# Gate and up strips of a SwiGLU block in pairs: seven block products in place of eight, in a float32 decoder kernel

## The chip, the cores and the metric

The kernel runs on one core of a Trainium2 chip. The core has a matrix engine (TensorE, PE in the profile; its loading of the stationary operand is shown apart as PEld), a vector engine (VectorE, DVE), an activation engine (ScalarE, ACT), GpSimd (POOL), and SyncE (SP), whose queue issues nearly all of this kernel's transfers. Every engine works through its own instructions in order and waits on semaphores where it needs another's result.

The metric is the device time of one execution in microseconds, as the median of the runs shown. A profile is one further execution, recorded instruction by instruction; its span is given with it.

## What is computed

Two layers of a decoder over 256 tokens with 2048 features, all in float32. Each layer has an input projection, two kinds of mixing heads, an output projection, a feed-forward block, and a gated per-layer input. What matters here is the feed-forward block:

```python
h = rms_norm(x, pre_ffn_gain[i])
f = (jax.nn.silu(h @ w_ffn_gate[i]) * (h @ w_ffn_up[i])) @ w_ffn_down[i]
x = x + rms_norm(f, post_ffn_gain[i])
```

`w_ffn_gate` and `w_ffn_up` are 2048 x 5632, `w_ffn_down` is 5632 x 2048. The kernel applies the gain to the transposed features before the product and the reciprocal root of the mean square after it.

## The kernel before

**Strips.** Every projection is computed in strips of 512 output columns. `strip` (line 294) goes over the features in chunks of 256, that is two blocks of 128; gate and up have 8 chunks. The 256 tokens are two row tiles of 128, t = 0 and t = 1, and each has a PSUM bank that accumulates over the whole strip (pool `pacc`, four banks). The stationary operand is a 128 x 128 block of the transposed features, the moving one a 128 x 512 block of weights.

**Three products for one.** A float32 operand is split in two parts of a shorter format (`F32R`), high and low, and a product is high x high + low x high + high x low: three matmuls, lines 306, 307 and 309. So a chunk costs 2 blocks x 3 matmuls for each row tile, 12 in all.

**Weights.** `fetch_w` (line 273) brings a chunk, 512 KB, into a raw tile (`wr`, four of them). `high` casts it on ACT into `wh` (line 281), and `load_w` subtracts on DVE into `wl` (line 291). There are eight `wh` and eight `wl`. A raw tile comes free when its subtraction is done; a `wh` when the last of its matmuls is.

**The feed-forward block.** 5632 columns are 11 strips. `gated(n)` (line 954) runs strip n of gate, then strip n of up. When a row tile of gate is complete, `done_gate` applies silu on ACT (line 960) into a tile `nat` (twelve of them); when up is complete, `done_up` multiplies on DVE (line 966), and the result is turned by a DVE transpose within blocks, a store to DRAM and four fetches back (`shuffled`, lines 227 to 240), and split again (lines 179 and 180) into the tile that the down projection reads. Groups of 2, 3, 3 and 3 strips are followed by the four strips of the down projection over just those columns, which add into SBUF (lines 991 and 993). Before the first group's down strips, strip 2 of gate and up is already done; the later groups have no such lead.

**What sets the order.** The code states dependencies and a program order. A planner then goes through the instructions with its own estimates of their time, and lays down a fixed order for each engine, the earlier in the program first among those that are ready and have a buffer. So an instruction on PE or ACT may be placed ahead of others that stand before it in the code. `later` and `tick` put work a number of chunks later in the program; `behind` ties an instruction to a point on its engine.

**Other tiles that the change touches.** `kT` and `vv` (keys and values, lines 542 and 543) are used in the mixing heads only, as is the tile with the tag `at` in `Rec`.

Of the kernel before, what the change touches and what calls it, by code (L numbers as in the profile page):

```python
# [8 lines left out]
F32 = mybir.dt.float32  # L9
F32R = mybir.dt.float32r  # L10
I32 = mybir.dt.int32
AF = mybir.ActivationFunctionType
ALU = mybir.AluOpType
AX = mybir.AxisListType

P = 128
SEQ = 256
NT = 2
# [6 lines left out]
W = 512  # L25
FF_GROUPS = (2, 3, 3, 3)
SKEW = 5
# [20 lines left out]
def decoder(ctx: ExitStack, tc: tile.TileContext, x, p, positions, w_in, attn_sinks,  # L48
# [9 lines left out]
    sp = ctx.enter_context(tc.tile_pool(name="sp", bufs=1))  # L58
# [3 lines left out]
    pacc = ctx.enter_context(tc.tile_pool(name="pacc", bufs=4, space=PSUM))  # L62
    pms = ctx.enter_context(tc.tile_pool(name="pms", bufs=4, space=PSUM))

    V, S, G, T = nc.vector, nc.scalar, nc.gpsimd, nc.tensor
# [7 lines left out]
    def later(n, fn):  # L73

        queue.append((clock[0] + n, fn))

    marks = {}

    @contextmanager
    def behind(*names):  # L80

        with ExitStack() as st:
            for n in names:
                st.enter_context(tc.issue_after(marks[n].ins))
            yield
# [9 lines left out]
    def tick():  # L95
        clock[0] += 1
        for gen in list(running):
            if next(gen, True):
                running.remove(gen)
        for item in [q for q in queue if q[0] <= clock[0]]:  # L100
            queue.remove(item)
            item[1]()

    def nat(shape=(P, W), dt=F32):
        return np_.tile(list(shape), dt, tag="nat", name="nat")

    def bank(shape=(P, W)):
        return pms.tile(list(shape), F32, tag="ms", name="ms")
# [20 lines left out]
    ps = bank()  # L129
    T.transpose(ps[:, 0:32], g0rows, ident[0:32, 0:32])  # L130
    S.preload_act_table(AF.Copy)
    first = V.tensor_copy(gT[:, 0:32], ps[:, 0:32])
# [4 lines left out]
    at = 0  # L137
    for g in (pre_ffn_gain, ple_gain, attn_out_gain, hgrn_out_gain):
        n = DEPTH * g.shape[1] // P
# [37 lines left out]
    def split(src, hi, lo):  # L177

        a = S.copy(hi, src)  # L179
        v = V.tensor_tensor(lo, src, hi.bitcast(F32), op=ALU.subtract)  # L180
        return a, v
# [35 lines left out]
    def shuffled(src, n=4, slow=True, ready=False):  # L217

        if ready:
            b = src
            V.transpose(b, b)  # L224
        else:
            b = nat((P, n * P))
            V.transpose(b.rearrange("p (q k j) -> p k q j", q=4, k=n),  # L227
                        src.rearrange("p (k q j) -> p k q j", k=n, q=4))
        m = dp.tile([4, 32, 4, n * 32], F32, tag="turn", name="turn")
        got = []  # L230

        def store():
            with behind("pe") if slow else nullcontext():
                nc.sync.dma_start(m.rearrange("a i q f -> (a i) (q f)"), b)

        def fetch():
            d = nat((P, n * P))
            with behind("pe") if slow else nullcontext():
                for q in range(4):
                    nc.sync.dma_start(d[q * 32:(q + 1) * 32].rearrange("i (a f) -> i a f", a=4),  # L240
                                      m[:, :, q].rearrange("a i f -> i a f"))
            got.append(d.rearrange("p (a k j) -> p k a j", a=4, k=n))
        if slow:
            later(1, store)
            later(2, fetch)
        else:
            store()
            fetch()
        return got
# [5 lines left out]
    def split_shuffled(d, gcols, hl, t):  # L255
        d, = d
        h, lo = (quarters(a[:, :, t * P:(t + 1) * P]) for a in hl)
        if gcols is None:
            split(d, h, lo)
            return  # L260
        for b in range(4):
            g = gcols[:, b:b + 1]
            marks["x"] = S.activation(h[:, b], d[:, b], AF.Copy, scale=g)  # L263
            V.scalar_tensor_tensor(lo[:, b], d[:, b], g, h[:, b].bitcast(F32),
                                   op0=ALU.mult, op1=ALU.subtract)

    def new_ck():
        return [xp.tile([P, 4, SEQ], F32R, tag="ck", name="ck", bufs=14) for i in range(2)]
# [4 lines left out]
    def fetch_w(w, c, col):  # L273
        raw = wpr.tile([P, 2, W], F32, tag="wr", name="wr")
        nc.sync.dma_start(raw, w[c * 2 * P:(c + 1) * 2 * P, col:col + W].rearrange(
            "(k p) n -> p k n", p=P))
        return raw

    def high(raw):
        hi = wps.tile([P, 2, W], F32R, tag="wh", name="wh")  # L280
        marks["hi"] = S.copy(hi, raw)  # L281
        return hi

    def load_w(w, c, col, raw=None, hi=None):

        if raw is None:
            raw = fetch_w(w, c, col)
        if hi is None:
            hi = high(raw)
        lo = wps.tile([P, 2, W], F32R, tag="wl", name="wl")  # L290
        marks["lo"] = V.tensor_tensor(lo, raw, hi.bitcast(F32), op=ALU.subtract)  # L291
        return hi, lo

    def strip(lhs, w, col, done, nch=8, row0=0, skew=0, psum=None, pre=None):

        ps = psum or [pacc.tile([P, W], F32, tag="acc", name=f"acc{t}") for t in range(NT)]
        ws = {}

        def part(t, c, lows=(0, 1)):
            hi, lo = ws[c]  # L300
            for k in range(2):
                kt = 2 * c + k
                xh, xl = (a[:, kt % 4, t * P:(t + 1) * P] for a in lhs[kt // 4])
                first, last = kt == 0, kt == 2 * nch - 1
                if 0 in lows:
                    T.matmul(ps[t], xh, hi[:, k], start=first, stop=False)  # L306
                    T.matmul(ps[t], xl, hi[:, k], start=False, stop=False)  # L307
                if 1 in lows:
                    marks[t, c] = marks["pe"] = T.matmul(ps[t], xh, lo[:, k], start=False,  # L309
                                                           stop=last)  # L310

        for i in range(nch + skew):
            ready = pre(i) if pre else ()
            if i < nch:
                with behind(("xh", 2 * i), ("xl", 2 * i)) if pre else nullcontext():
                    ws[i] = load_w(w, row0 // (2 * P) + i, col, *ready)
                if pre and i == 0:
                    for t in range(NT):
                        part(t, i, (0,))
                    for t in range(NT):  # L320
                        part(t, i, (1,))
                    tick()
                    continue
                part(0, i)
                if i == nch - 1:
                    done(0, ps[0])
            if i >= skew:
                part(1, i - skew)
            tick()
        done(1, ps[1])  # L330

    def load_gain(g, col):
        b = np_.tile([P, W], F32, tag="gB", name="gB", bufs=2)
        nc.sync.dma_start(b, g[col:col + W].partition_broadcast(P))
        return b
# [147 lines left out]
    xT = [new_ck() for c in range(4)]  # L483
# [51 lines left out]
    for l in range(DEPTH):  # L535
# [3 lines left out]
        attn = [new_ck(), new_ck()]  # L539
        mix = {0: attn[0], 1: attn[1]}  # L540
        qT = {}
        kT = sp.tile([P, 2, SEQ], F32, tag="kT", name="kT")
        vv = sp.tile([P, NT, 256], F32, tag="vv", name="vv")
        ao = [sp.tile([P, 2, W], F32, tag="CD"[t], name=f"ao{t}") for t in range(NT)]
        ssa = new_ss("ssa")
        rot = {}
# [385 lines left out]
        xT = [new_ck() for c in range(4)]  # L932
        mg = []
        for s in range(4):
            gB = load_gain(post_mix_gain[l], s * W)

            def done(t, ps, s=s, gB=gB):
                if t == 0:
                    mg.append(sp.tile([P, NT, W], F32, tag="ABCD"[s], name=f"mg{s}"))
                square_sum(ps, ssm[t][:, s:s + 1])  # L940
                V.tensor_tensor(mg[s][:, t], ps, gB, op=ALU.mult)
                if s == 3:
                    post_norm(mg, ssm, t, ss, xT, gain_cols(32, l, 16), 4)
# [6 lines left out]
        ff0 = 0  # L950
        macc = [None] * 4
        hidden = []

        def gated(n):
            col = n * W
            gate = {}

            def done_gate(t, ps):
                gate[t] = nat()
                S.activation(gate[t], ps, AF.Silu, scale=rx2(t)[:, 0:1])  # L960

            hl = new_ck()
            hidden.append(hl)

            def done_up(t, ps):
                V.scalar_tensor_tensor(gate[t], ps, rx2(t)[:, 0:1], gate[t],  # L966
                                       op0=ALU.mult, op1=ALU.mult)
                d = shuffled(gate[t], slow=False)
                later(3, lambda: split_shuffled(d, None, hl, t))

            strip(xT, w_ffn_gate[l], col, done_gate, skew=SKEW if n == 0 else 0)
            strip(xT, w_ffn_up[l], col, done_up)

        for gi, glen in enumerate(FF_GROUPS):

# [3 lines left out]
            last = gi == len(FF_GROUPS) - 1  # L979
            if last:  # L980
                nxT = [new_ck() for c in range(4)]
            for s in range(4):
# [16 lines left out]
                if last and s == 2:  # L999
                    pT2 = sp.tile([P, 2, 2, SEQ], F32R, tag="at", name="pT2")  # L1000
                    pT = [pT2[:, 0], pT2[:, 1]]
                    for t in range(NT):
# [4 lines left out]
                      skew=4 if last and s == 3 else 0)  # L1007
            ff0 += glen
        xT, ss = nxT, nss
# [34 lines left out]
        xT, ss = nxT, nss  # L1044
# [31 lines left out]
```

## Time and profile before

| | |
|---|---|
| median of 3 runs | 2444.12 us (2442.08 to 2444.22) |
| span of the profiled execution | 2443.7 us |
| PE busy | 2425.5 us, 99% of the span, 11251 matmuls |
| weight loading busy (PEld) | 2007.7 us, 82% |
| DVE busy | 1483.3 us, 61% |
| ACT busy | 1180.7 us, 48% |
| POOL busy | 98.7 us, 4% |
| mean DMA rate | 204 GB/s |
| weight chunks of gate and up fetched | 176 and 176, 512 KB each |

A row of the profile's groups names the line of the kernel, the engine, the operation, the tile written and the tiles read, the shapes and the count; behind the bar stand the busy time in us, the mean of one in ns, and the time for which the engine sat idle just before, with what ended it. The ends of matmuls are modelled and consecutive ones overlap, so the duration in a matmul's row is longer than the spacing of two. A timeline row gives the start in us, the time, and the idle time before in brackets. In the rows of waits, the numbers are us in total, times, and the longest.

### The profile page before, as it was taken

The page shows a single profiled execution, that of the slowest core. Times are in us where ns is not written, and L with a number is a line of the kernel's source. Part 1 is how long each engine was busy: PE and PEld are TensorE (multiplying, and loading weights), DVE is VectorE, ACT ScalarE, POOL GpSimd, SP SyncE. Part 2 cuts the span into 40 slices and gives each one's busy share as a digit, 9 for nine tenths or more (in the row PEclk, how much of TensorE's full clock was granted, in tenths as well). Part 3 has the DMA queues.
Part 4 walks back from the last instruction along what each step waited for, and adds up shares of the span by engine and source line. Part 5 has one row for each costly group of instructions (what it writes and reads, how often), then busy time and mean ns, then how long its engine had stood idle before and what let it go on. Part 6 is the DMA issues. An engine that isn't in the chain of part 4 may idle for free.

```text
span 2443.7 us, 30841 instructions
## 1 busy us (share of the span) xinstructions
PE 2425.5 (99%) x11251; PEld 2007.7 (82%) x11251; DVE 1483.3 (61%) x1979; ACT 1180.7 (48%) x1666; POOL 98.7 (4%) x213
## 2 busy tenths in 40 slices
PE   9999999999999999999999999999999999999999
PEld 7788888888888888888888888888888888888887
DVE  7687856554555555557666878565545555555674
ACT  6464546444444444446555554464444444344462
POOL 3100001000000000001010000010000000000010
PEclk9999999999999999999999999999999999999999
DMA  7656565776667766765766565657767676677753
GB/s 257 210 164 216 189 189 167 231 223 199 214 207 209 213 208 196 225 218 168 244 214 198 177 204 182 201 189 214 225 193 228 192 213 211 208 209 211 223 174 129
DMA packets 299351, 497.59 MB, mean 204 GB/s; under 512 B 23456, under 2 KB 69440, under 8 KB 299200
## 3 DMA queue, kind: packets, MB, share of 16 engines
q1 hardware_dynamic: 298896, 495.54, 65.9%
q8 instruction: 88, 1.44, 0.2%
q14 instruction: 63, 0.52, 0.1%
q10 hardware_dynamic: 240, 0.07, 0.0%
q0 software_dynamic: 64, 0.02, 0.0%
HBM read 470.38 MB, written 25.17 MB: 203 GB/s over the span
## 4 chain that ended last, share of the span: by engine, by line
PE 92%; DVE 4%; DMA 2%; issue 1%; ACT 1%; POOL 0%; SPq 0%; DVEq 0%; ACTq 0%; POOLq 0%
PE acc L309 29%; PE acc L306 29%; PE acc L307 29%; DMA wr<-in_w_in_dram 1%; DVE wl L291 1%; PE ms L682 1%; PE ms L794 1%; PE ms L201 1%; PE ms L624 0%; ACT wh L281 0%; PE ms L860 0%; DMA nat<-turn 0%; DVE x L342 0%; PE ms L887 0%; DMA turn<-nat 0%
## 5 line engine op out<-in xcount | busy, mean ns | idle before, releaser
L291 DVE TENSOR_TENSOR wl<-wr,wh 128x1024 fp32r<-128x1024 f32 x840 | 1023.4, 1222 | 825.6 <-ACT wh L281 821.8
L281 ACT CAST wh<-wr 128x1024 fp32r<-128x1024 f32 x840 | 882.5, 1054 | 1098.6 <-PE acc L307 885.6
L306 PE MATMUL acc<-wh,ck 128*128 128x512 f32 x3328 | 1302.8, 392 | 0.8 <-ACT ck L179 0.8
L309 PE MATMUL acc<-wl,ck 128*128 128x512 f32 x3328 | 1297.5, 390 | 2.1 <-DVE wl L291 1.9
L307 PE MATMUL acc<-wh,ck 128*128 128x512 f32 x3328 | 1298.5, 390 | 0.3 <-DVE ck L180 0.2
L309 PEld LDWEIGHTS acc<-wl,ck 128*128 128x128 f32 x3328 | 625.2, 188 | 134.1 <-DVE wl L291 4.6
L307 PEld LDWEIGHTS acc<-wh,ck 128*128 128x128 f32 x3328 | 625.6, 188 | 131.6 <-DVE ck L180 2.3
L306 PEld LDWEIGHTS acc<-wh,ck 128*128 128x128 f32 x3328 | 625.3, 188 | 130.2 <-ACT ck L179 3.1
L165 POOL TENSOR_TENSOR tiny<-ssf 128x1 f32<-128x1 f32 x4 | 1.9, 470 | 1351.8 <-ACT junk L175 1351.8
L210 DVE SCALAR_TENSOR_TENSOR ck<-ms,gT,ck 128x128 fp32r<-128x128 f32 x152 | 42.6, 342 | 4.5 <-ACT ck L208 4.2
L208 ACT ACTIVATE ck<-ms,gT 128x128 fp32r<-128x128 f32 x152 | 43.3, 371 | 1.5 <-PE ms L201 1.4
L180 DVE TENSOR_TENSOR ck<-nat,ck 128x512 fp32r<-128x512 f32 x52 | 35.7, 686 | 2.0 <-ACT ck L179 1.9
L993 DVE TENSOR_TENSOR macc<-acc,macc 128x512 f32<-128x512 f32 x48 | 33.0, 687 | 5.8 <-PE acc L309 5.2
L960 ACT ACTIVATE nat<-acc,ry 128x512 f32<-128x512 f32 x44 | 30.2, 686 | 10.7 <-PE acc L309 10.7
L179 ACT CAST ck<-nat 128x512 fp32r<-128x512 f32 x52 | 32.2, 618 | 5.7 <-DVE nat L191 3.9
L227 DVE STREAM_TRANSPOSE nat<-nat 128x512 f32<-128x512 f32 (+1 forms) x48 | 32.7, 681 | 2.6 <-POOL nat L569 2.6
L966 DVE SCALAR_TENSOR_TENSOR nat<-acc,ry,nat 128x512 f32<-128x512 f32 x44 | 32.4, 747 | 0.1
L175 ACT ACTIVATE junk<-x 128x512 f32<-128x512 f32 x48 | 30.9, 643 | 3.1 <-DVE x L1027 2.6
L224 DVE STREAM_TRANSPOSE nat<-nat 128x512 f32<-128x512 f32 x32 | 22.6, 706 | 10.6 <-POOL nat L569 5.7
L654 ACT ACTIVATE nat<-nat,tiny 128x128 f32<-128x128 f32 x64 | 24.9, 392 | 4.1 <-DVE tiny L651 4.0
L263 ACT ACTIVATE ck<-nat,gT 128x128 fp32r<-128x128 f32 x72 | 22.5, 391 | 7.6 <-DMA nat<-turn 7.4
L569 POOL TENSOR_TENSOR nat<-nat 128x256 f32<-128x256 f32 (+1 forms) x24 | 20.5, 876 | 115.0 <-DVE nat L562 55.6
(196 smaller groups left out, 900.9 us busy)
## 6 DMA issues: line engine op xcount, KB each, us to landing
wr<-in_w_in_dram SPq DMA_DIRECT2D x176, 512.0 KB, 4.6
wr<-in_w_ffn_gate_dram SPq DMA_DIRECT2D x176, 512.0 KB, 3.8
wr<-in_w_ffn_up_dram SPq DMA_DIRECT2D x176, 512.0 KB, 4.4
wr<-in_w_ffn_down_dram SPq DMA_DIRECT2D x176, 512.0 KB, 4.4
wr<-in_w_out_dram SPq DMA_DIRECT2D x64, 512.0 KB, 3.7
wr<-in_w_ple_gate_dram SPq DMA_DIRECT2D x64, 512.0 KB, 4.7
turn<-nat SPq DMA_DIRECT2D x86, 256.0 KB, 2.6
nat<-turn SPq DMA_DIRECT2D x344, 64.0 KB, 3.0
```

What stands on the lines that cost most here:

```text
L179: a = S.copy(hi, src)
L180: v = V.tensor_tensor(lo, src, hi.bitcast(F32), op=ALU.subtract)
L208: S.activation(h[:, b], ps[:, b], AF.Copy, scale=gcols[:, b:b + 1])
L210: V.scalar_tensor_tensor(lo[:, b], ps[:, b], gcols[:, b:b + 1], h[:, b].bitcast(F32), op0=ALU.mult, op1=ALU.subtract)
L227: V.transpose(b.rearrange("p (q k j) -> p k q j", q=4, k=n), src.rearrange("p (k q j) -> p k q j", k=n, q=4))
L281: marks["hi"] = S.copy(hi, raw)
L291: marks["lo"] = V.tensor_tensor(lo, raw, hi.bitcast(F32), op=ALU.subtract)
L306: T.matmul(ps[t], xh, hi[:, k], start=first, stop=False)
L307: T.matmul(ps[t], xl, hi[:, k], start=False, stop=False)
L309: marks[t, c] = marks["pe"] = T.matmul(ps[t], xh, lo[:, k], start=False, stop=last)
L966: V.scalar_tensor_tensor(gate[t], ps, rx2(t)[:, 0:1], gate[t], op0=ALU.mult, op1=ALU.mult)
L993: V.tensor_tensor(m, ps, m, op=ALU.add)
```

## The change

Strip 0 of gate and up stays as it is. From strip 1 on, `gated` calls a new function `paired`, which computes the two strips together. Chunks 0 and 1 of the features, for both row tiles and both weights, form a product of 2 x 2 blocks: row tile by chunk on one side (each block 128 tokens x 256 features), chunk by weight on the other (256 features x 512 columns). It is computed with seven products of sums of blocks (Winograd's form of Strassen's scheme) in place of eight products of blocks. Chunks 2 to 7 are added in the ordinary way.

The sums on the features' side (`sx`) are the same for all strips; `mixed` makes them once a layer, on DVE, and splits them into high and low. The sums on the weights' side are made for each strip on DVE, in place in the raw tiles: four subtractions, which use the raw tiles of both chunks of both weights. Partial results that are needed twice are copied from PSUM to `nat` tiles on ACT (`saved`), and three of the four outputs are completed by an addition on DVE, with one more addition among the partial results. `paired` uses all four banks of `pacc`.

The feature sums go into the tiles with the tags `kv` and `at`; for that, `kT` and `vv` become the two halves of one tile with the tag `kv`.

```diff
+    def mixed(lhs):
+        hi = sp.tile([P, 4, 2, P], F32R, tag="kv", name="sh")
+        lo = sp.tile([P, 4, 2, P], F32R, tag="at", name="sl")
+        a = []
+        for c in range(2):
+            k = slice(2 * c, 2 * c + 2)
+            full = nat((P, 2, SEQ))
+            V.tensor_tensor(full, lhs[0][:, k].bitcast(F32), lhs[1][:, k].bitcast(F32), op=ALU.add)
+            a.append([full[:, :, t * P:(t + 1) * P] for t in range(NT)])
+        s = [nat((P, 2, 2, P)) for _ in range(2)]
+        s1, s2, s3, s4 = s[0][:, 0], s[0][:, 1], s[1][:, 0], s[1][:, 1]
+        for dst, p, q, op in ((s1, a[0][1], a[1][1], ALU.add), (s2, s1, a[0][0], ALU.subtract),
+                              (s3, a[0][0], a[0][1], ALU.subtract), (s4, a[1][0], s2, ALU.subtract)):
+            V.tensor_tensor(dst, p, q, op=op)
+        for i in range(2):
+            split(s[i], hi[:, 2 * i:2 * i + 2], lo[:, 2 * i:2 * i + 2])
+        return hi, lo
+
+    def paired(lhs, sx, wa, wb, col, done_a, done_b, nch=8, row0=0):
...
+        def acc(ps, x, w, first=False, last=False):
+            hi, lo = w
+            for k in range(2):
+                xh, xl = x(k)
+                T.matmul(ps, xh, hi[:, k], start=first and k == 0, stop=False, skip_group_check=True)
+                T.matmul(ps, xl, hi[:, k], start=False, stop=False, skip_group_check=True)
+                marks["pe"] = T.matmul(ps, xh, lo[:, k], start=False, stop=k == 1, skip_group_check=True)
...
+        def saved(ps):
+            b = nat()
+            S.copy(b, ps)
+            return b
...
+        r11, r12, r22, r21 = raw(wa, 0), raw(wb, 0), raw(wb, 1), raw(wa, 1)
+        a = psum("acca")
+        acc(a, block(0, 0), parts(r11), first=True)
+        p1 = saved(a)
+        sub(r11, r12, r11)
+        c = psum("accc")
+        acc(c, combo(1), parts(r11), first=True)
+        p5 = saved(c)
+        tick()
+        sub(r12, r22, r12)
+        e = psum("acce")
+        acc(e, block(1, 0), parts(r21), first=True)
+        w22 = parts(r22)
+        sub(r22, r22, r11)
+        acc(a, combo(2), parts(r22))
+        u2 = saved(a)
+        tick()
+        acc(c, combo(4), w22)
+        ws = {}
+
+        def std(ps, t, k, first=False):
+            acc(ps, block(k, t), ws[k], first=first, last=k == nch - 1)
+        ws[2] = load_w(wa, base + 2, col)
+        std(e, 0, 2)
+        tick()
+        acc(a, combo(3), parts(r12))
+        V.tensor_tensor(p5, a, p5, op=ALU.add)
+        ws[3] = load_w(wa, base + 3, col)
+        std(e, 0, 3)
+        tick()
+        sub(r21, r21, r22)
+        ws[4] = load_w(wa, base + 4, col)
+        std(e, 0, 4)
+        acc(a, block(1, 1), parts(r21))
+        tick()
+        for i in range(5, nch):
+            ws[i] = load_w(wa, base + i, col)
+            std(e, 0, i)
+            if i == nch - 1:
+                V.tensor_tensor(p1, e, p1, op=ALU.add)
+                done_a(0, p1)
+            std(a, 1, i - 3)
+            tick()
+        for i in range(nch - 3, nch):
+            std(a, 1, i)
+        done_a(1, a)
+        tick()
+        d = psum("accd")
+        for i in range(2, nch):
+            ws[i] = load_w(wb, base + i, col)
+            std(c, 0, i)
+            if i == nch - 1:
+                V.tensor_tensor(u2, c, u2, op=ALU.add)
+                done_b(0, u2)
+            std(d, 1, i, first=i == 2)
+            tick()
+        V.tensor_tensor(p5, d, p5, op=ALU.add)
+        done_b(1, p5)
...
-        kT = sp.tile([P, 2, SEQ], F32, tag="kT", name="kT")
-        vv = sp.tile([P, NT, 256], F32, tag="vv", name="vv")
+        kv4 = sp.tile([P, 2, 2, SEQ], F32, tag="kv", name="kv")
+        kT, vv = kv4[:, 0], kv4[:, 1]
...
-            strip(xT, w_ffn_gate[l], col, done_gate, skew=SKEW if n == 0 else 0)
-            strip(xT, w_ffn_up[l], col, done_up)
+            if n == 0:
+                strip(xT, w_ffn_gate[l], col, done_gate, skew=SKEW)
+                strip(xT, w_ffn_up[l], col, done_up)
+                return
+            if n == 1:
+                sx.append(mixed(xT[0]))
+            paired(xT, sx[0], w_ffn_gate[l], w_ffn_up[l], col, done_gate, done_up)
```

In the text below w11, w21 are chunks 0 and 1 of the gate weight, w12 and w22 those of up; w11', w12', w22' and w21' are the sums that `sub` leaves in r11, r12, r22 and r21, in that order of names.

More of the change, by code (lines that the diff above doesn't have):

```diff
@@ new lines, in paired, with block, get, combo @@
+    def paired(lhs, sx, wa, wb, col, done_a, done_b, nch=8, row0=0):
+        def block(c, t):
+            def get(k):
+                kt = 2 * c + k
+                return tuple(a[:, kt % 4, t * P:(t + 1) * P] for a in lhs[kt // 4])
+            return get
+        def combo(i):
+            return lambda k: (sx[0][:, i - 1, k], sx[1][:, i - 1, k])
+        def acc(ps, x, w, first=False, last=False):
[5 more added lines that the diff above has]
+                marks["pe"] = T.matmul(ps, xh, lo[:, k], start=False, stop=k == 1, skip_group_check=True)
+        def psum(name):
+            return pacc.tile([P, W], F32, tag="acc", name=name)
+        def saved(ps):
+            b = nat()
+            S.copy(b, ps)
+            return b
+        base = row0 // (2 * P)
+        def raw(w, c):
+            return fetch_w(w, base + c, col)
+        def parts(r):
+            return load_w(None, 0, 0, raw=r)
+        def sub(dst, p, q):
+            V.tensor_tensor(dst, p, q, op=ALU.subtract)
+        r11, r12, r22, r21 = raw(wa, 0), raw(wb, 0), raw(wb, 1), raw(wa, 1)
[55 more added lines that the diff above has]
+        done_b(1, p5)
@@ L952, in decoder @@
         hidden = []
+        sx = []
         def gated(n):
```

## Prediction

> **What bounds the kernel now.** I read the page from the top: busy time by engine, then the chain that ended last, then the costliest groups. In a row of the groups the numbers after the bar are busy time in us, mean ns of one, and the idle time just before, with what ended it.
>
> ```profile
> span 2443.7 us, 30841 instructions
> PE 2425.5 (99%) x11251; PEld 2007.7 (82%) x11251; DVE 1483.3 (61%) x1979; ACT 1180.7 (48%) x1666; POOL 98.7 (4%) x213
> ...
> PE 92%; DVE 4%; DMA 2%; issue 1%; ACT 1%; POOL 0%; SPq 0%; DVEq 0%; ACTq 0%; POOLq 0%
> ...
> L291 DVE TENSOR_TENSOR wl<-wr,wh 128x1024 fp32r<-128x1024 f32 x840 | 1023.4, 1222 | 825.6 <-ACT wh L281 821.8
> L281 ACT CAST wh<-wr 128x1024 fp32r<-128x1024 f32 x840 | 882.5, 1054 | 1098.6 <-PE acc L307 885.6
> L306 PE MATMUL acc<-wh,ck 128*128 128x512 f32 x3328 | 1302.8, 392 | 0.8 <-ACT ck L179 0.8
> L309 PE MATMUL acc<-wl,ck 128*128 128x512 f32 x3328 | 1297.5, 390 | 2.1 <-DVE wl L291 1.9
> L307 PE MATMUL acc<-wh,ck 128*128 128x512 f32 x3328 | 1298.5, 390 | 0.3 <-DVE ck L180 0.2
> ```
>
> PE is busy all the time, the chain is PE for 92%, and its 9984 strip products wait 3.2 us in all. ACT, which casts the weights, idles 885.6 us for PE to give a `wh` buffer back. There are eight of them, so a cast that waits for PE is eight weight tiles ahead of it. PE is the bound; ACT and DVE follow with room to spare.
>
> The stretch that the change touches is a gate and an up strip together. Its period shows on DVE, between two calls of line 966 (one pair of calls for each such pair of strips), and the busy times in just that stretch follow:
>
> ```profile
> 449.07 1.54 DVE L966 SCALAR_TENSOR_TENSOR nat<-acc,ry,nat 128x512 f32<-128x512 f32 x2
> ...
> 492.59 1.47 DVE L966 SCALAR_TENSOR_TENSOR nat<-acc,ry,nat 128x512 f32<-128x512 f32 x2
> ```
> ```profile
> core 0: us, PE busy (x) PEld busy (x) DVE busy (x) ACT busy (x) POOL busy (x), PEclk, DMA share, GB/s
> 449.07:492.59 43.52, 43.52 (x194) 36.05 (x193) 23.33 (x23) 19.19 (x20) 0.00 (x0) 1.00 0.72 219
> ```
>
> By the code a pair has 2 weights x 8 chunks x 2 row tiles x 2 blocks x 3 products = 192 matmuls (the row's 194 count two that overlap its edges). 43.52 / 192 = 0.2267 us each, at a granted clock of 1.00. I call the six matmuls of one chunk and one row tile a step: 6 x 0.2267 = 1.36 us.
>
> **What is removed.** Chunks 0 and 1 of both strips were 2 x 2 x 2 = 8 steps and become 7. A pair has 31 steps instead of 32, 186 matmuls. It applies to strips 1 to 10 of each layer (strip 0 keeps the old path), so 20 pairs: 20 x 1.36 = **27.2 us off PE**.
>
> The Trainium skill, page "TensorE: Matmul & The Clock Gate", section "Back-to-back issue gap", gives about 131 ns as the sustained spacing of products with 512 columns; by it the 120 removed matmuls would be worth 15.7 us (an estimate from that page). The row above measures 227 ns for these very matmuls, and it decides.
>
> **What is added.** Prices of the new operations, from the nearest rows:
>
> ```profile
> L180 DVE TENSOR_TENSOR ck<-nat,ck 128x512 fp32r<-128x512 f32 x52 | 35.7, 686 | 2.0 <-ACT ck L179 1.9
> ...
> L993 DVE TENSOR_TENSOR macc<-acc,macc 128x512 f32<-128x512 f32 x48 | 33.0, 687 | 5.8 <-PE acc L309 5.2
> ...
> L179 ACT CAST ck<-nat 128x512 fp32r<-128x512 f32 x52 | 32.2, 618 | 5.7 <-DVE nat L191 3.9 <-DMA nat<-turn 1.6
> L966 DVE SCALAR_TENSOR_TENSOR nat<-acc,ry,nat 128x512 f32<-128x512 f32 x44 | 32.4, 747 | 0.1
> ...
> L991 ACT COPY macc<-acc 128x512 f32<-128x512 f32 x16 | 9.4, 585 | 3.2 <-PE acc L309 3.2
> ...
> L762 DVE TENSOR_TENSOR q<-q,f 128x512 f32<-128x512 f32 x12 | 8.4, 702 | 3.3 <-PE ms L860 3.3
> ...
> L820 DVE TENSOR_TENSOR f<-f 128x256 f32<-128x256 f32 (+1 forms) x8 | 3.5, 443 | 0.0
> ```
>
> - Weight sums in place, four a pair, 128x1024 f32: not in the trace. Line 291 has the size and the engine, 1.22; twice the in-place 128x512 of line 762 is 1.40. I take 1.22, the nearer; the other end costs 4 x 0.18 = 0.7 us of DVE a pair.
> - Three more cast-and-subtract splits a pair (19, not 16): 3 x 1.05 on ACT, 3 x 1.22 on DVE.
> - Three copies of a PSUM tile on ACT (line 991, 0.585) and four adds PSUM + SBUF on DVE (line 993, 0.687). Gate and up then read two of four results from SBUF; line 179 against line 991 (0.618 from SBUF, 0.585 from PSUM) says that this costs nothing to speak of, either way.
> - `mixed`, once a layer: two sums of 512 elements, four of 256, two splits: 2 x 0.69 + 4 x 0.44 + 2 x 0.69 = 4.5 us of DVE and 1.2 of ACT. It can run any time in the 43.5 us of strip 0, in which DVE idles some 20. Uncovered it would cost 2 x 5.7 = 11 us; I take nothing.
> - `kT` and `vv` become one tile of the same bytes: nothing moves.
>
> DVE per pair: 23.3 + 3.7 + 4.9 + 2.7 = 34.6 of 42.16 us (82%). ACT: 19.2 + 3.2 + 1.8 = 24.2 (57%). Neither becomes the bound as a total. The bytes fetched are the same 16 tiles.
>
> **Whether PE stays fed.** The sums hold all four raw tiles (`wr`) at once, and the first ten steps use ten different weights, each for one step only. These rows give the time of a fetch:
>
> ```profile
> DMA to landing us min/median/max: 3.6/4.1/5.9
> ```
> ```profile
> SPq L275 <- DVE wl L291: 489.1, 233, 6.5
> ```
>
> The second says that fetches already spend their time waiting for DVE to give a raw tile back, as they will now. I walk one pair, t = 0 at its first step. The steps use, in order, w11, w11', w21, w22', w22, chunk 2, w12', chunk 3, chunk 4, w21', then chunks 5, 2, 6, 3, 7, 4 and so on; step n starts at 1.36 n. In the previous pair's second half PE gives back one `wh` every two steps, 2.72 us (line 281 has eight), so casts can start: w11 and w11' before -13.6, w21 -13.6, w22 -10.9, w22' -8.2, chunk 2 -5.4, w12' -2.7, chunk 3 at 0, chunk 4 at 1.4, w21' at 2.7.
>
> - w22 is split by -10.9 + 1.05 + 1.22 = -8.6; the sum w22' then ends at -7.4 and frees the raw tile of w11. Chunk 2 is fetched: landing -3.3, cast -2.2, split -1.0. It is used at 6.8: margin 7.8 us.
> - w22' is split by -7.4 + 2.27 = -5.1, the sum w21' ends at -3.9 and frees w22's raw tile: chunk 3 lands at 0.2, split by 2.5, used at 9.5: margin 7.
> - Chunk 4 takes chunk 2's raw tile at -1.0: lands 3.1, split by 5.4, used at 10.9: margin 5.5.
>
> With the slowest landing in the row, 5.9, each of these loses 1.8 us and still holds. DVE's work from t = 0 to 13.6: seven splits 8.6, three adds 2.1 (two end the previous pair), two of line 966 1.5, two turns 1.4, two of line 180 1.4: 15.0 us, 1.4 more than there is, paid from a margin of 5.5.
>
> PSUM is tighter. The copy of the first product must end before that bank is used again at step 3, two steps or 2.72 us after; the same holds for the second product (step 4) and the sum at step 3 (step 6). With 0.585 for the copy and a cast of 1.05 in progress, 1.1 us is left. The add after step 6 (0.69, plus a split of 1.22 in progress) leaves 0.8. So I count these at nothing too, with the cover named.
>
> What is not free is the end of a group, where the down strips use the hidden block just made. They already wait a little, in the first layer's FFN alone:
>
> ```profile
> PEld acc L306 <- ACT ck L179: 1.2, 4, 0.4
> PEld acc L307 <- DVE ck L180: 1.0, 3, 0.5
> ```
>
> The block now comes one add (0.69) later. Three of four groups a layer need it at once: 6 x 0.69 = 4.1 us, between nothing (PE takes another strip's steps) and 8 us (both adds in series). I take 4.
>
> **Sum.** 2443.7 - 27.2 + 4.1 = 2420.6 by the span; the runs' median is 0.4 above it: **2421 us**, 0.9% faster.
>
> **Rivals.**
>
> 1. *A copy stands behind a late cast on ACT (slower).* ACT runs in order; this is how its copies of results sit between casts today:
>
> ```profile
> 468.60 1.05 ACT L281 CAST wh<-wr 128x1024 fp32r<-128x1024 f32 x1 [1.15 <-PE acc L307]
> 470.19 0.69 ACT L960 ACTIVATE nat<-acc,ry 128x512 f32<-128x512 f32 x1 [0.53 <-PE acc L309]
> 471.32 1.05 ACT L281 CAST wh<-wr 128x1024 fp32r<-128x1024 f32 x1 [0.44 <-PE acc L307]
> ```
>
> For it: a new copy queued behind chunk 4's cast (landing 3.1, cast done 4.2) ends at 4.8, but its bank is wanted at 4.08: PE waits 0.7, or 2.5 with the slowest landing. Behind each copy then wait the next casts, and behind those DVE's splits. Against it: the order now in use puts line 960 where PE has just finished, 0.53 us of idle. Three copies a pair at 0.7 to 2.5 are 2.1 to 7.5 us a pair; the gain is gone from (27.2 - 4.1) / 20 = 1.16 a pair. At 2.6, the first two copies late at the median landing and the third halfway to the slowest (0.7 + 0.7 + 1.2): 2421 + 52 = **2473 us**; with all three at 2.5 it is 2571. Chance 16%.
>
> 2. *The fetches come late in part.* SP issues nothing while four raw tiles are held, from about -14 (the previous pair's last chunk is split, before w11) to -7.4, then fetches come close together. A tile takes 0.524 MB x 0.72 / 219 GB/s = 1.7 us of all the DMA engines, by the row of the pair; behind two others a fetch lands 3.4 later than alone, and if it is also one of the slowest (1.8 more) the margin of 5.5 is spent. About 0.7 us a pair, half a step, then shows: 2421 + 14 = **2435 us**. Against it: the margins of the walk. Chance 10%.
>
> 3. *The steps saved come back as waits*, that is 1.36 us a pair through any of the tight places, PSUM included: **2444 us**. The change then removes PE work without removing time. Chance 7%.
>
> **How the numbers follow.** Forecast 67%, its own range 2416 to 2429: below, if the groups' ends cost nothing; above, if `mixed` shows or the dearer sums do. Rivals 16, 10 and 7%. A measurement of this kernel can tell about 0.2%, 4.9 us, from no change. Faster by more than that (below 2439): the forecast, rival 2 mostly, 75%. Within it: rival 3 and the edges of 1 and 2, 10%. Slower: 15%. The range must leave out no more than 2 in 10: 2415 to 2446 leaves rival 1, and what little lies below.
>
> **What would show it.** PE's count falls by 120 to 11131; nothing is added on PE. The groups of the new matmul line must have idle times of a few us, as lines 306 to 309 now have. The stretch between two gate-up ends must be 42.2 us, with DVE busy about 34.6 and ACT 24.2 in it. Weight sums should read 1.2 us, copies 0.6, adds 0.7. Wrong if PE waits on ACT's copies (rival 1), on splits after a long SP gap (rival 2), or if the pair's period stays at 43.5.

## The result, and the profile after

The change made the kernel slower: 2522.3 us (median of 4 runs, 2518.4 to 2526.2) against 2444.1 (4 runs, 2442.1 to 2444.2), a ratio of 1.032 with a 95% interval of 1.031 to 1.034. The prediction was 2421 us, with a range of 2415 to 2446.

The head of the page after, and the groups that answer to those of before (busy us, mean ns | idle before and what ended it):

```profile
span 2516.7 us, 31204 instructions
...
PE 2433.4 (97%) x11131; PEld 1990.3 (79%) x11131; DVE 1697.4 (67%) x2215; ACT 1267.0 (50%) x1790; POOL 100.0 (4%) x213
...
L291 DVE TENSOR_TENSOR wl<-wr,wh 128x1024 fp32r<-128x1024 f32 x900 | 1088.9, 1220 | 608.3 <-ACT wh L281 594.6
L281 ACT CAST wh<-wr 128x1024 fp32r<-128x1024 f32 x900 | 938.0, 1052 | 988.0 <-PE acc L307 362.5
...
L387 DVE TENSOR_TENSOR wr<-wr 128x1024 f32<-128x1024 f32 x80 | 97.9, 1224 | 5.8 <-DMA wr<-in_w_ffn_up_dram 3.5
...
L180 DVE TENSOR_TENSOR ck<-nat,ck 128x512 fp32r<-128x512 f32 x52 | 35.9, 690 | 70.3 <-ACT ck L179 70.2
```

The 120 matmuls are gone (11131), the weight sums (line 387) cost 1.224 us each, and the 60 more splits are there. But PE, whose strip products before waited 3.2 us in all, is busy for 8 us longer with fewer matmuls, and line 180, the split of the hidden block, has 70 us of idle DVE ahead of it. The waits of PE, longest first (us in total, times, longest):

```profile
PE accc L366 <- ACT sh L179: 24.4, 2, 12.3
PE acce L366 <- ACT wh L281: 17.1, 11, 2.6
PE acca L366 <- ACT nat L375: 16.5, 17, 1.6
PE acce L368 <- DVE wl L291: 7.0, 15, 0.5
```

All four are in products of the new function. They wait, row by row, for the split of the feature sums (`sh`), for a cast of weights, for the copy out of PSUM that frees the bank (line 375), and for a split of weights.

I took the starts of all strip matmuls from the timeline and summed what each interval between two neighbours has over 0.2267 us (leaving out what is under 0.02). I call that the excess. It is 18 us before and 118 after: 100 more, less the 27.2 removed, is 73, and the span grew by 73.0. So this sum accounts for the loss, and it can be laid to the pairs:

| pairs | number | excess, each |
|---|---|---|
| strip 1 of each layer, after strip 0 | 2 | 14.2 and 15.0 us |
| strips 3, 5 and 8, after the down strips of a group | 6 | 0.2 to 0.8 us |
| strips 2, 4, 6, 7, 9 and 10, after another pair | 12 | 3.7 to 8.6 us, 70 in all |

Where a pair has no gate-up pair just before it, the prediction's walk holds. Two of them in one table of stretches, strip 6 and strip 5 of the first layer (columns as in the prediction):

```profile
core 0: us, PE busy (x) PEld busy (x) DVE busy (x) ACT busy (x) POOL busy (x), PEclk, DMA share, GB/s
792.73:838.69 45.96, 43.62 (x187) 34.60 (x186) 33.28 (x34) 23.40 (x26) 0.00 (x0) 1.00 0.67 206
750.07:792.73 42.66, 42.46 (x187) 34.83 (x186) 29.96 (x29) 22.18 (x24) 0.00 (x0) 1.00 0.64 197
```

Strip 5 takes 42.66 us where 42.16 were forecast, strip 6 takes 45.96. What differs shows on ACT. First strip 6, whose first step ends at 794.1 (start us, us, what, idle before):

```profile
797.93 1.06 ACT L281 CAST wh<-wr 128x1024 fp32r<-128x1024 f32 x1 [0.41 <-DMA wr<-in_w_ffn_gate_dram]
802.91 0.62 ACT L179 CAST ck<-nat 128x512 fp32r<-128x512 f32 x1 [3.92 <-DMA nat<-turn]
803.43 0.58 ACT L375 COPY nat<-acca 128x512 f32<-128x512 f32 x1
803.91 0.59 ACT L375 COPY nat<-accc 128x512 f32<-128x512 f32 x1
805.52 1.05 ACT L281 CAST wh<-wr 128x1024 fp32r<-128x1024 f32 x1 [1.03 <-PE acca L367]
```

And strip 5, whose first step ends at 751.4:

```profile
752.93 1.05 ACT L281 CAST wh<-wr 128x1024 fp32r<-128x1024 f32 x1 [1.78 <-DMA wr<-in_w_ffn_gate_dram]
753.88 0.57 ACT L375 COPY nat<-acca 128x512 f32<-128x512 f32 x1
754.36 0.59 ACT L375 COPY nat<-accc 128x512 f32<-128x512 f32 x1
754.84 2.95 ACT L281 CAST wh<-wr 128x1024 fp32r<-128x1024 f32 x3
```

In strip 5 the copy of the first product comes 2.5 us after its step. In strip 6 it comes 9.3 us after, behind line 179: ACT stands 3.92 us for the return of strip 5's hidden block from DRAM. In the program the copy stands *ahead* of that split; the planner has put it behind. The feature sums in strip 1 sit in the same place. ACT and DVE there, one view each:

```profile
457.45 0.62 ACT L179 CAST ck<-nat 128x512 fp32r<-128x512 f32 x1 [5.56 <-DMA nat<-turn]
457.98 0.58 ACT L375 COPY nat<-acca 128x512 f32<-128x512 f32 x1
```
```profile
458.10 0.69 DVE L180 TENSOR_TENSOR ck<-nat,ck 128x512 fp32r<-128x512 f32 x1 [4.33 <-ACT ck L179]
458.71 1.29 DVE L340 TENSOR_TENSOR nat<-ck 128x512 f32<-128x512 f32 x2
```

Line 340 reads features that were complete by 420 us, and DVE had time before (it idles 5.4 us between 420 and 440), but it runs at 458.7, again just behind strip 0's split.

What the copies and the feature sums share is the tag of the tile that they write, `nat`. The turned hidden block uses it too: a tile before the store and one after the return. **Theory A**: the planner hands out the tiles of a tag in program order, so a copy cannot be planned before the previous strip's return has its tile, that is, before the plan has SP issue it. (It can hold only of the planner's own times: in the run the fetches for the second row tile of strip 5 start at 803.61, just after the copy.) The rivals were **B**, raw tiles (fetches late, since the sums hold all four), and **C**, too much DVE work in the first ten products.

### The profile page after: what moved, and what is told of

It reads as the page before. It is cut to its first block, busy times and chain, and to the rows that moved or that the text cites. A ratio compares the mean times of both kernels' runs of the same rounds, so it can differ in the third digit from the quotient of the medians.

```text
span 2516.7 us, 31204 instructions
## 1 busy us (share of the span) xinstructions
PE 2433.4 (97%) x11131; PEld 1990.3 (79%) x11131; DVE 1697.4 (67%) x2215; ACT 1267.0 (50%) x1790; POOL 100.0 (4%) x213
## 5 line engine op out<-in xcount | busy, mean ns | idle before, releaser
L306 PE MATMUL acc<-wh,ck 128*128 128x512 f32 x2048 | 802.8, 393 | 0.4 <-ACT ck L179 0.4
L309 PE MATMUL acc<-wl,ck 128*128 128x512 f32 x2048 | 799.2, 391 | 2.1 <-DVE wl L291 1.9
L307 PE MATMUL acc<-wh,ck 128*128 128x512 f32 x2048 | 800.2, 391 | 0.3 <-DVE ck L180 0.3
L309 PEld LDWEIGHTS acc<-wl,ck 128*128 128x128 f32 x2048 | 384.7, 188 | 84.4 <-DVE wl L291 4.8
L307 PEld LDWEIGHTS acc<-wh,ck 128*128 128x128 f32 x2048 | 385.1, 188 | 80.4 <-DVE ck L180 2.3
L306 PEld LDWEIGHTS acc<-wh,ck 128*128 128x128 f32 x2048 | 384.8, 188 | 79.2 <-ACT ck L179 1.0
L366 PE MATMUL acca<-wh,ck 128*128 128x512 f32 x320 | 130.4, 407 | 0.9
L367 PE MATMUL acca<-wh,ck 128*128 128x512 f32 x320 | 128.5, 401 | 0.0
L368 PE MATMUL acca<-wl,ck 128*128 128x512 f32 x320 | 127.9, 400 | 0.0
L366 PE MATMUL acce<-wh,ck 128*128 128x512 f32 x280 | 111.1, 397 | 17.1 <-ACT wh L281 17.1
L368 PE MATMUL acce<-wl,ck 128*128 128x512 f32 x280 | 112.2, 401 | 7.0 <-DVE wl L291 7.0
L367 PE MATMUL acce<-wh,ck 128*128 128x512 f32 x280 | 109.5, 391 | 0.0
L366 PE MATMUL accc<-wh,ck 128*128 128x512 f32 x240 | 93.4, 389 | 0.0
L367 PE MATMUL accc<-wh,ck 128*128 128x512 f32 x240 | 93.4, 389 | 0.0
L366 PE MATMUL accd<-wh,ck 128*128 128x512 f32 x240 | 93.4, 389 | 0.0
L367 PE MATMUL accd<-wh,ck 128*128 128x512 f32 x240 | 93.4, 389 | 0.0
```

The lines of the kernel that those rows point to most:

```text
L366: T.matmul(ps, xh, hi[:, k], start=first and k == 0, stop=False, skip_group_check=True)
L367: T.matmul(ps, xl, hi[:, k], start=False, stop=False, skip_group_check=True)
L368: marks["pe"] = T.matmul(ps, xh, lo[:, k], start=False, stop=k == 1, skip_group_check=True)
```

## The experiments

**Tiles of their own for the copies.** Same total room: three tiles out of nat's twelve.

```diff
-    np_ = ctx.enter_context(tc.tile_pool(name="np", bufs=12))
+    np_ = ctx.enter_context(tc.tile_pool(name="np", bufs=9))
...
-            b = nat()
+            b = np_.tile([P, W], F32, tag="sv", name="sv", bufs=3)
             S.copy(b, ps)
```

> Theory A: nat tiles are handed out in program order, so the three copies out of PSUM (and the feature sums) cannot be planned before the previous strip's turned result has its own nat tile, that is, before its return from DRAM is issued; ACT then takes the split of that result, which waits for the return, ahead of the copies, and PE waits behind both. Here the copies get three tiles of a tag of their own (nat 12 to 9), nothing else changes. A expects the copy to stand right after the first product, the ten pairs that follow another pair to lose under 1.5 us each where they lost 3 to 7, and the sums of the features to be as late as before: about 50 us less than the changed kernel, 2465 to 2480. Theory B, raw tiles: fetches are late because the sums hold all four raw tiles, and the copies are late only because ACT waits for casts; B expects no change beyond 8 us (2514 to 2530). Theory C, DVE has too much to do for the first ten products: no change either.

Measured: 2459.1 us (4 runs; ratio to before 1.007, 1.005 to 1.008), 63 us less than the changed kernel. ACT at the start of strip 6, whose first step now ends at 788.2:

```profile
789.17 1.05 ACT L281 CAST wh<-wr 128x1024 fp32r<-128x1024 f32 x1 [1.28 <-DMA wr<-in_w_ffn_gate_dram]
790.13 0.57 ACT L375 COPY sv<-acca 128x512 f32<-128x512 f32 x1
790.61 0.59 ACT L375 COPY sv<-accc 128x512 f32<-128x512 f32 x1
791.08 2.01 ACT L281 CAST wh<-wr 128x1024 fp32r<-128x1024 f32 x2
792.99 0.59 ACT L375 COPY sv<-acca 128x512 f32<-128x512 f32 x1
796.18 1.05 ACT L281 CAST wh<-wr 128x1024 fp32r<-128x1024 f32 x1 [2.60 <-DMA wr<-in_w_ffn_gate_dram]
797.14 0.61 ACT L179 CAST ck<-nat 128x512 fp32r<-128x512 f32 x1
```

The copy comes 1.9 us after its step, three copies and four casts stand ahead of the split, and the split waits for nothing. The twelve pairs that follow a pair (ten in the expectation, a miscount) lose 0 to 1.3 us. The time is 6 us below the range that A gave; B and C gave no gain. Strip 1 still loses its 14 us.

**Feature sums earlier in the program.**

```diff
                 strip(xT, w_ffn_gate[l], col, done_gate, skew=SKEW)
+                sx.append(mixed(xT[0]))
                 strip(xT, w_ffn_up[l], col, done_up)
                 return
-            if n == 1:
-                sx.append(mixed(xT[0]))
```

> The feature sums stand in the program between strip 0 of gate and strip 0 of up, so their nat tiles come before those of strip 0's turned result. A: the 12.3 us wait of each layer's first pair goes, with the slower clock behind it: 2522 less 28 to 36, 2486 to 2494; the later pairs stay as they are. B and C: the sums were late because DVE or ACT had no time for them; moved earlier they take it from strip 0 and the gain is under 10 us.

Measured: 2486.3 us (1.018, 1.017 to 1.020), 36 us less. The two strips 1 go from 14 and 15 us of excess to 1.6 and 2.2; the pairs after a pair still lose some 3 to 7. As A has it.

**A fifth raw tile.**

```diff
-    wpr = ctx.enter_context(tc.tile_pool(name="wpr", bufs=4))
+    wpr = ctx.enter_context(tc.tile_pool(name="wpr", bufs=5))
...
-    np_ = ctx.enter_context(tc.tile_pool(name="np", bufs=12))
+    np_ = ctx.enter_context(tc.tile_pool(name="np", bufs=10))
```

> Five raw tiles in place of four (nat 12 to 10 for the room). B: one fetch more can be in flight while the sums hold four; waits on casts and splits behind fetches go, 30 to 60 us less than the changed kernel. A: the copies and the feature sums still wait for the nat tiles: within 10 us of 2522.

Measured: 2495.7 us (1.021, 1.019 to 1.023), 27 us less. Neither theory had this: too much for A alone, too little for B. The pairs kept their pattern (strip 1 about 14, those after a pair 2.6 to 7.4), so it did not replace A; a part of the gain lies outside the pairs, since the first pair starts 7.7 us earlier. The later runs take this up.

**No turn.**

```diff
-                d = shuffled(gate[t], slow=False)
+                d = [gate[t].rearrange("p (a k j) -> p k a j", a=4, k=4)]
```

> Left out: the turn of the hidden block (the transposes on DVE, the store and the four fetches back); the split reads the product tile directly, so the down projection gets wrongly ordered features and the times are of less work on DVE (1.4 us a strip) and on the queues. A: no nat tile waits for a return and no split on ACT waits for DRAM, so both the copies and the feature sums come on time: 2430 to 2450. B and C: fetches of weights and DVE's sums are as they were, 2505 to 2520.

Measured: 2425.9 us (0.993, 0.992 to 0.995), a little under A's band. With the return away, both losses all but go (about 2 us are left in each strip 1), with four raw tiles and all the sums in place. This and the first run put B and C down as main causes.

**Both edits.**

> Both edits together: tiles of their own for the copies, feature sums between strip 0 of gate and of up. Theory A (order of allocation in the nat tag is the whole loss): the two gains add, 63 + 36 under the changed kernel, 2424 us, and that is the 27.2 us of removed matmuls less about 0.4 us a pair; granted clock 0.998 or more. Against it, that each edit only moved the same wait and the rest comes back at the next tight place (casts behind fetches): 2435 to 2450.

Measured: 2431.2 us (5 runs; 0.995, 0.994 to 0.996), between the two forecasts. The gains add to 91 of the expected 99. The period of a pair is now the forecast one (strips 1 and 6, first layer):

```profile
core 0: us, PE busy (x) PEld busy (x) DVE busy (x) ACT busy (x) POOL busy (x), PEclk, DMA share, GB/s
446.41:488.57 42.16, 42.16 (x188) 34.91 (x186) 30.83 (x31) 23.19 (x26) 0.00 (x0) 1.00 0.69 222
768.34:810.50 42.16, 42.16 (x187) 34.87 (x186) 32.19 (x33) 23.36 (x26) 0.00 (x0) 1.00 0.69 224
```

What was left stands mostly at the ends of groups:

```profile
PE acc L306 <- ACT ck L179: 6.4, 5, 2.3
PE ms L740 <- ACT qT L712: 2.5, 1, 2.5
PE acca L366 <- ACT sv L375: 1.9, 5, 0.8
```

**The turned block's tiles apart instead.** The copies and feature sums stay where they were; only the two tiles of the hidden block's turn leave the tag.

```diff
-    np_ = ctx.enter_context(tc.tile_pool(name="np", bufs=12))
+    np_ = ctx.enter_context(tc.tile_pool(name="np", bufs=8))
...
-            b = nat((P, n * P))
+            b = nat((P, n * P)) if slow else tn()
...
-            d = nat((P, n * P))
+            d = nat((P, n * P)) if slow else tn()
```

(`tn` gives a tile of a tag of its own, of which there are four.)

> The other way round: copies and feature sums stay in nat and where they were in the program; only the two tiles of the turned hidden block (before the store and after the return) get a tag of their own, four tiles, and nat goes from 12 to 8. If it is the order in which one tag hands out its tiles, this one edit takes both losses away, the copies' and the feature sums': 2424 to 2432. If it is the number of tiles, eight for nat is worse than twelve: over 2500. If it is the place of the feature sums in the program, their 12 us wait stays: about 2460.

Measured: 2428.5 us (0.994, 0.993 to 0.995). This is the sharpest of the runs. It has no more room, eight tiles in nat where there were twelve, and not one instruction moved in the program, and both losses are gone together: strips 1 have no excess, strips 2 at most 1.7. The feature sums now start in strip 0's time, and in strip 6 the copy comes 1.9 us after its step, ahead of the split that still waits for the return (line numbers are three higher here):

```profile
427.12 0.69 DVE L343 TENSOR_TENSOR nat<-ck 128x512 f32<-128x512 f32 x1
```
```profile
770.69 0.57 ACT L378 COPY nat<-acca 128x512 f32<-128x512 f32 x1
...
777.79 0.62 ACT L179 CAST ck<-tn 128x512 fp32r<-128x512 f32 x1 [1.50 <-DMA tn<-turn]
```

So it is who shares the tag; where `mixed` is called matters only through that. That `nat` simply had too few tiles is not excluded by this run alone: by the code a pair now asks it for five tiles where it asked for nine, and no run gave it more. Against that stands the run with a fifth raw tile: with ten `nat` tiles in place of twelve, the twenty pairs lost 92 us, where they had lost 102. That the planner goes by program order within a tag is inferred from this; the trace shows only the order that it laid down.

**Both edits and five raw tiles.**

> Both edits and a fifth raw tile (nat 9 to 7). If raw tiles held by the sums still cost PE anything once the copies are on time, this is faster than the kernel with both edits by 3 us or more; I expect none of it, within 3 us of that kernel.

Measured: 2403.4 us (0.984, 0.983 to 0.985), 28 us less than with four; I had expected nothing. Every one of the twenty pairs is without excess. Of the 28, 7.5 us fall before the first pair and 4.8 between the last pair's start of one layer and the first's of the next; in the feed-forward blocks the groups' ends improve most (from strip 7 to strip 8 of the first layer 108.1 us, 111.8 before). The waits on line 179 fall from 6.4 us to 1.0.

**No weight sums.** With four raw tiles and both edits:

```diff
         def sub(dst, p, q):
-            V.tensor_tensor(dst, p, q, op=ALU.subtract)
+            return
```

> Both edits, and left out: the four in-place weight sums of each pair, so the products use the weights themselves and the output is not the reference's. DVE does 4.9 us less in each pair and no cast waits for a sum. If the sums are hidden, as the prediction costed them, the time is that of the kernel with both edits within 3 us; if DVE or the raw tiles are near the limit, 10 us or more less.

Measured: 2415.4 us (0.989, 0.987 to 0.990), 16 us less than the kernel with both edits. So with four raw tiles the sums are not free: 80 of them cost 16 us, a sixth of their own 98 us of DVE time, and 7 of the 16 lie in the pairs. With five raw tiles their cost in the pairs is gone, though DVE does the same work. That speaks for B's raw tiles as a second, smaller cause, and against C.

**The kernel before with five raw tiles, and the best one again.** The first is the kernel before with the fifth raw tile's two edits, and the second is the kernel with both edits and the fifth tile, unchanged.

> The kernel before the change with five raw tiles (nat 12 to 10). If the fifth raw tile helps the kernel with both edits only because the weight sums hold raw tiles, this is within 4 us of the kernel before. If it helps the other stages, whatever the change, this is 15 to 25 us faster than the kernel before.

> The fastest kernel so far, beside the one before with the same five raw tiles on the same chip: their difference is what seven products in place of eight are worth when nothing waits. By the removed matmuls, 20 pairs of 1.36 us: 27 us, 22 to 28.

Measured: 2433.0 us (5 runs; 0.996, 0.995 to 0.997) and 2403.8 us (5 runs; 0.984, 0.983 to 0.986). The fifth raw tile is worth 9.9 us to the kernel before, between the two forecasts for it, and this part of its gain owes nothing to the change: ACT's waits for the input projection's weights, 114.7 us in the kernel before, are 34.0 with it. With the raw tiles equal, seven products in place of eight are worth 29.2 us, by medians; the removed matmuls are 27.2. The kernel with both edits and five raw tiles is the fastest of all, 1.6% under the kernel before.

## Why the prediction was wrong

The direction was wrong, and two terms of the sum failed, both costed at nothing for a cover that was there but was not used.

- *"It can run any time in the 43.5 us of strip 0 ... I take nothing"* (`mixed`). DVE's idle time was there, as was the input. In the planner's order its tile was not to be had in that time (inferred, as said at the run with the turned block's tiles apart). The uncovered price was put at 11 us in all; PE waited 24.4 us, since the sums came behind a return from DRAM as well, and ran slowly after. Moving the call gave 36 us back.
- *"So I count these at nothing too"* (the copies out of PSUM). The walk gave them 1.1 us of margin by asking what ACT is doing when the product ends. It did not ask when the planner could place the copy, nor what tile the copy writes. The code says `nat`, whose tiles the hidden block uses too; no step of the walk looked at that. Own tiles gave 63 us back.
- *Rival 1*, a copy stuck on ACT, had the right engine and the right instruction, a price of 2473 to 2571 us, and 16%. What it stands behind was wrong: not a cast of chunk 4 that is late from DRAM, but the split of the previous strip's hidden block, and the loss shows only where there is one. That 2522 lies between the two prices is luck. The row quoted against it, line 960 between two casts with 0.53 us of idle, writes a `nat` tile as well, but in the program it comes a whole strip after the last hidden block. In the kernel before, both casts of that block on line 179 had ended by 467.5 us, without a wait, when line 960 ran at 470.19. It was the wrong row to judge the copies by.
- *Right*: 120 matmuls at 0.2267 us (29.2 us at equal raw tiles, 27.2 forecast); the pair's period of 42.16 us, to the hundredth where nothing waits; the prices of a sum (1.224, forecast 1.22), a copy (0.58 to 0.59, forecast 0.585) and an add (0.69); ACT 22.2 to 23.4 us in a pair (24.2). DVE's 34.6 was high: 30.0 to 33.3.
- *The groups' ends*: 4.1 us, between 0 and 8. With both edits PE's weight loads wait 8.7 us for line 179 and 2.7 for line 180, where it was 3.1 and 2.3: 6.0 more.
- *Rival 2*, late fetches, is there but small: the weight sums cost 16 us with four raw tiles once the order is mended (14 was its price). The margins of the walk took each landing alone.

From the forecast 2421 to 2522 are 101 us. Of these 91 are the tag, shown by the two edits; the remaining 10 lie within what the raw tiles and the sums cost. No run parts the 91 into waits and slow matmuls; in the changed kernel's trace, of the 102 us of excess in the pairs, 78 lie in the 66 intervals in which PE waits and 24 in matmuls that follow one another without a wait, but more slowly. Nor was it tried to move the hidden block's split alone. With the copies in their own tiles it still waits for its return, 27.7 us in all where it was 94.0, and the pairs that follow a pair lose 1.3 us at most, so its own share is small at most in that order of work.

## What to carry to other kernels

When new short-lived results are put into a pool that others use, ask for each tile who stands ahead of it in the program under the same tag and what *that* one waits for; a free buffer and an idle engine are no cover if an earlier taker of the tag is waiting on a round trip through DRAM. Results on PE's path belong in a tag of their own, even at the price of fewer tiles elsewhere. And when a change takes several input tiles at once, price one input tile more, on the kernel before as well: here it gave 10 us without the change and 28 with it.

## What the runs showed of the hardware

PE's clock came into it, which no step had foreseen. The stretches around the 12.3 us wait of strip 1 in the changed kernel:

```profile
core 0: us, PE busy (x) PEld busy (x) DVE busy (x) ACT busy (x) POOL busy (x), PEclk, DMA share, GB/s
440.00:449.00 9.00, 9.00 (x41) 7.44 (x41) 6.49 (x7) 3.83 (x4) 0.00 (x0) 1.00 0.49 132
449.00:461.00 12.00, 0.72 (x4) 0.26 (x2) 6.92 (x11) 2.42 (x4) 0.00 (x0) 0.61 0.77 243
461.00:464.00 3.00, 2.17 (x4) 1.46 (x5) 2.54 (x5) 1.76 (x3) 0.00 (x0) 0.50 0.14 30
464.00:468.00 4.00, 4.00 (x16) 3.26 (x15) 1.64 (x2) 2.70 (x4) 0.00 (x0) 0.83 0.00 0
468.00:472.00 4.00, 4.00 (x20) 3.30 (x19) 3.26 (x3) 2.41 (x4) 0.00 (x0) 1.00 0.81 221
```

After the wait the granted clock is 0.50. PE starts again at 461.8, and the mean of 0.83 from 464 to 468 puts the return to full rate at about 465.4, 3.6 us later. The Trainium skill, page "TensorE: Matmul & The Clock Gate", section "What's actually happening", has half rate after an idle window of about 3.4 us, and full rate after about as long of work. The return agrees. The fall came sooner than that: the first two rows below put it 2.0 us after PE went idle.

```profile
core 0: us, PE busy (x) PEld busy (x) DVE busy (x) ACT busy (x) POOL busy (x), PEclk, DMA share, GB/s
449.72:451.74 2.02, 0.00 (x0) 0.00 (x0) 1.49 (x2) 0.90 (x1) 0.00 (x0) 1.00 0.95 346
451.74:461.83 10.09, 0.00 (x0) 0.00 (x0) 5.28 (x10) 1.92 (x5) 0.00 (x0) 0.50 0.70 203
513.18:516.59 3.41, 1.87 (x7) 1.13 (x7) 1.07 (x2) 1.59 (x3) 0.00 (x0) 1.00 0.84 252
516.59:520.00 3.41, 3.41 (x9) 2.67 (x9) 0.70 (x1) 1.53 (x2) 0.00 (x0) 0.50 1.00 297
```

Another place is further off. In strip 2 PE waits 0.26 and then 1.28 us (the brackets), and runs at half rate all the same, matmuls 0.43 us apart from 516.7 on:

```profile
513.61 0.50 PE L368 MATMUL acce<-wl,ck 128*128 128x512 f32 x1 [0.26 <-DVE wl L291]
...
516.09 0.50 PE L366 MATMUL acca<-wh,sh 128*128 128x512 f32 x1 [1.28 <-ACT nat L375]
516.42 0.48 PE L367 MATMUL acca<-wh,sl 128*128 128x512 f32 x1
516.70 0.63 PE L368 MATMUL acca<-wl,sh 128*128 128x512 f32 x1
517.13 0.63 PE L366 MATMUL acca<-wh,sh 128*128 128x512 f32 x1
517.56 0.63 PE L367 MATMUL acca<-wh,sl 128*128 128x512 f32 x1
```

So a short wait can cost more than itself: no idle stretch here came near 3.4 us, and by the rule of that section the clock should have stayed. The last two rows above show what went before it: in the 3.41 us ahead of the fall PE was busy for 1.87, and the half rate then lasted 3.41 us, though PE was busy all through. Why it fell was not tried.
